# A fixed issue order on TensorE, and a pinned copy, in a decoder trunk of two layers

## The chip, the cores and the metric

The kernel runs on one core of one Trainium2 chip. The time is device microseconds of one execution. A core has TensorE (PE in the profile, with its weight loads as PEld), VectorE (DVE), ScalarE (ACT), GpSimd (POOL) and SyncE (SP), each with an instruction queue of its own.

## The reference

The kernel computes two pre-norm residual layers and a final norm on 256 tokens of width 2048, in float32. Layer 0 projects to an RWKV-7 group of 16 heads of 64 and to a differential-attention group of 8 heads, and layer 1 is a gated MLP that mixes positions in chunks of 128. Each is followed by a SwiGLU FFN of width 5632. Cut to what matters here:

```python
for i in range(DEPTH):
    h = rms_norm(x, mix_norm[i])
    if i % 2 == 0:
        z = h @ ev_w_in[j]
        y_a = rwkv7_time_mix(z[..., :RWKV_COLS], ...)
        y_b = diff_attention(z[..., RWKV_COLS:], ...)
        y = jnp.concatenate([y_a, y_b], axis=-1) @ ev_w_out[j]
    else:
        z = h @ od_w_in[j]
        y = chunked_sgu(z, ...) @ od_w_out[j]
    x = x + y
    x = x + swiglu(rms_norm(x, ffn_norm[i]), ...)
return rms_norm(x, final_norm)

def step(S, inp):                       # the scan in rwkv7_time_mix, per token
    r_t, w_t, k_t, v_t, a_t, b_t = inp
    sa = einsum('bhvk,bhk->bhv', S, a_t)
    S = S * w_t + sa[..., None] * b_t + v_t[..., None] * k_t
    return S, einsum('bhvk,bhk->bhv', S, r_t)
```

## The kernel before

**Main matmuls.** All weights come as a stream in the order of `stream()`. `weights()` (L241) loads the next piece on SP's queue and splits it into `hi` (a cast on ScalarE, L255) and `lo` (the rest, on VectorE, L256), one piece ahead of its use in the text, into five buffers each. `proj_a` (L288) multiplies 256 rows by 256 columns at a time, in layer 0's input projection with matmuls of 256 columns (L314 to L316), elsewhere with 512 and 256 (L302, L306). `proj_b` (L327) turns the operands round, in steps of 128 rows with six matmuls of 416 or 512 columns (L335 to L337).

**Side work.** The RWKV group is worked in four quarters of four heads (`quarter`, L537), written as a Python generator; rotary positions, attention, the mixing matrices and the layer norm of layer 1 are generators too. After each step of a projection `tick()` (L272) advances the generators, 1.3 steps a tick for the quarters and 1.1 for the others. So the text of the program interleaves main matmuls with small steps, and `pause(n)` puts n empty steps in between. The lines of a quarter in their order: LoRA products L545 and L546; norm of k through L562; its transposes L582; products of a chunk L619; a round trip of 16x16 diagonal blocks through DRAM on POOL's queue (L626 out, L628 back into `DB`, L629 sets ones); the bonus product L636; masks L647 and L654; transposes of v L668 and a product L681; thirteen empty steps; then the substitution that inverts the diagonal blocks on VectorE, from the copy L692 into `inv` over 15 rounds of a product L696 (`sub`) and a sum L697; the products L705 to L718 that use it; the scan over four chunks (L742, L747, L754); and the output norm with L805 and L811. L380 and L387 are the sums over partitions and the transposes of a token norm (`Norm.end`), with the Newton steps of `rsqrt` (L176) between them on VectorE. `norm.end(True)`, at L476 and L985, issues both; without `True` only the sums are issued.

**What sets the order.** The program is written in the Tile framework. A planner at compile time orders each engine's queue by an estimate of when operands are there: of what it believes ready it takes the instruction that comes first in the text. On each engine the order is then fixed, and an instruction that has to wait on the chip holds back those behind it. Before, all five queues are ordered like this.

Of the kernel before, what the change touches and what calls it, by code (L numbers as in the profile page):

```python
# [130 lines left out]
def trunk_kernel(  # L131
# [15 lines left out]
    nc = tc.nc  # L147
    V, S, T, G = nc.vector, nc.scalar, nc.tensor, nc.gpsimd

    cpool = ctx.enter_context(tc.tile_pool(name="cpool", bufs=1))  # L150
    wpool = ctx.enter_context(tc.tile_pool(name="wpool", bufs=4))
    pool = ctx.enter_context(tc.tile_pool(name="pool", bufs=1))
# [17 lines left out]
    def small(shape, tag, bufs=2):  # L170
        return pool.tile(list(shape), F32, tag=tag, name=nm(tag), bufs=bufs)
# [21 lines left out]
    def bc(ap, axis, n):  # L193
        a = ap.unsqueeze(axis)
        shape = list(a.shape)
        shape[axis] = n
        return a.to_broadcast(shape)

    def r3(ap, k):
        return ap.rearrange("p (k f) -> p k f", k=k)  # L200
# [33 lines left out]
    def cc(name):  # L234
        i, o, w = CON[name]
        return ctile[i][:, o : o + w]
# [300 lines left out]
    def quarter(q, r_, k_, v_):  # L537
# [151 lines left out]
        yield from pause(Y7)  # L689

        inv = r3(small([128, 128], "inv", 1), 8)
        V.tensor_copy(inv, bc(cc("i16"), 1, 8))  # L692
        d4 = diag.rearrange("p (u r s) -> p u r s", u=8, r=16)
        for r in range(1, 16):
            t = r3(small([128, 128], "sub"), 8)[:, :, 0 : r + 1]
# [230 lines left out]
    def ap_(g, i):  # L926
# [3 lines left out]
        else:  # L930
            res[g, i] = []
            start(f"r{g}{i}", rope(t, res[g, i]))

    start("q0", quarter(0, *rkv(0, acc)))
    ap_(0, 0)
    start("q1", quarter(1, *rkv(1)))
    ap_(0, 1)
    ap_(0, 2)
    start("q2", quarter(2, *rkv(2)))
    start("q3", quarter(3, *rkv(3)))  # L940
    for i in range(3):
# [191 lines left out]
```

## Time and profile before

| | us |
|---|---|
| median of 3 runs (2349.5 to 2353.93) | 2350.4 |
| profiled execution | 2349.51 |
| its span | 2347.7 |
| TensorE busy in it | 2291.3 |
| VectorE busy in it | 1531.8 |
| ScalarE busy in it | 1197.4 |
| mean granted TensorE clock in it | 0.992 |

A busy time is the union of an engine's instructions. A wait is the idle time of an engine in front of an instruction, put down to the semaphore that came last. A timeline row has the start and the length of a run of like instructions, then `output<-inputs` by the program's names, and in brackets the idle time before it. The clock is a share of TensorE's full clock, of whose two levels (1.2 and 2.4 GHz) the windows show a mean. The input projection of layer 0 runs until about 530 us of the span, its output projection and FFN to about 1280, and layer 1 thereafter.

### The profile page before, as it was taken

The numbers are of one execution on the slowest core, as the hardware profiler recorded it, in microseconds if no ns is written. First come the engines' busy times: TensorE is split into PE (matmuls) and PEld (weight loads), VectorE is DVE, ScalarE is ACT, GpSimd is POOL, SyncE is SP. The second block draws the span as 40 slices with busy tenths as digits, with TensorE's granted clock in tenths as the row PEclk, the third lists the DMA queues.
The fourth block names the chain that finished last, engine by engine and source line by source line (L and its number), as shares of the span: only waits on it lengthen the run. The fifth ranks groups of instructions, "written<-read, shape, count | busy, mean of one in ns | idle before, by whom it ended". The sixth has DMA issues, their size and how long they took to land.

```text
span 2347.7 us, 39701 instructions
## 1 busy us (share of the span) xinstructions
PE 2291.3 (98%) x14878; PEld 2008.8 (86%) x14878; DVE 1531.8 (65%) x2845; ACT 1197.4 (51%) x2230; POOL 66.4 (3%) x96
## 2 busy tenths in 40 slices
PE   8898989899999999999999999999999999999997
PEld 8887887688888888888888888888888888888887
DVE  7667776688766666665555558776666666665554
ACT  6445544556555555554444455555555555544443
POOL 0000000002000000000000000010000000000000
PEclk9999999999999999999999999999999999999999
DMA  6544344435566665656666765566666666656664
GB/s 217 144 135 123 117 124 146 115 113 185 183 189 189 188 189 188 189 189 188 189 189 188 244 194 176 177 188 181 192 190 189 187 188 191 190 189 189 189 189 135
DMA packets 121105, 414.08 MB, mean 176 GB/s; under 512 B 14160, under 2 KB 18384, under 8 KB 120400
## 3 DMA queue, kind: packets, MB, share of 16 engines
q1 hardware_dynamic: 113664, 401.00, 55.1%
q0 software_dynamic: 2112, 4.46, 0.9%
q10 hardware_dynamic: 5136, 6.09, 0.8%
q8 instruction: 116, 1.90, 0.3%
q14 instruction: 77, 0.63, 0.1%
HBM read 409.14 MB, written 2.36 MB: 175 GB/s over the span
## 4 chain that ended last, share of the span: by engine, by line
PE 77%; DVE 2%; issue 1%; DMA 1%; ACT 0%; POOL 0%; DVEq 0%; POOLq 0%; ACTq 0%
PE acc L302 46%; PE acc L306 24%; PE acc L314 1%; PE acc L315 1%; PE acc L316 1%; PE acc L337 1%; PE acc L336 1%; PE acc L335 1%; DVE lo L256 1%; ACT hi L255 0%; DMA AT<-in_w_s 0%; PE sm L1026 0%; DMA st<-in_wts 0%; PE sm L742 0%; DVE xres L1043 0%
## 5 line engine op out<-in xcount | busy, mean ns | idle before, releaser
L256 DVE TENSOR_TENSOR lo<-st,hi 128x512 fp32r<-128x512 f32 (+1 forms) x1520 | 1048.6, 694 | 618.6 <-ACT hi L255 613.8
L255 ACT CAST hi<-st 128x512 fp32r<-128x512 f32 (+1 forms) x1520 | 927.3, 618 | 947.3 <-PE acc L302 606.6
L302 PE MATMUL acc<-H,hi 128*128 128x512 f32 x3560 | 901.2, 393 | 0.0
L302 PEld LDWEIGHTS acc<-H,hi 128*128 128x128 f32 x3560 | 639.2, 189 | 113.3 <-issue 0.3
L306 PEld LDWEIGHTS acc<-H,lo 128*128 128x128 f32 x3560 | 486.2, 190 | 44.4 <-DVE lo L256 9.3
L306 PE MATMUL acc<-H,lo 128*128 128x256 f32 x3560 | 501.5, 283 | 9.1 <-DVE lo L256 9.1
L316 PE MATMUL acc<-H,lo 128*128 128x256 f32 x488 | 141.7, 290 | 14.6 <-DVE lo L256 14.5
L314 PE MATMUL acc<-H,hi 128*128 128x256 f32 x488 | 144.1, 295 | 8.4 <-ACT hi L255 8.4
L315 PE MATMUL acc<-H,hi 128*128 128x256 f32 x488 | 140.9, 289 | 0.0
L336 PE MATMUL acc<-lo,H 128*128 128x512 f32 (+1 forms) x320 | 126.1, 394 | 6.5 <-DVE lo L256 6.5
L335 PE MATMUL acc<-hi,H 128*128 128x512 f32 (+1 forms) x320 | 129.6, 405 | 0.0
L337 PE MATMUL acc<-hi,H 128*128 128x512 f32 (+1 forms) x320 | 125.7, 393 | 0.0
L316 PEld LDWEIGHTS acc<-H,lo 128*128 128x128 f32 x488 | 96.1, 197 | 15.9 <-DVE lo L256 15.5
L302 PE MATMUL acc<-AT,hi 128*128 128x512 f32 x400 | 105.7, 396 | 0.0
L314 PEld LDWEIGHTS acc<-H,hi 128*128 128x128 f32 x488 | 96.0, 197 | 11.2 <-ACT hi L255 8.4
L302 PE MATMUL acc<-RB,hi 128*128 128x512 f32 x392 | 101.7, 392 | 0.0
L324 DVE TENSOR_TENSOR TR<-acc,TA 128x512 f32<-128x512 f32 x96 | 66.0, 688 | 54.3 <-ACT TA L323 54.3
L315 PEld LDWEIGHTS acc<-H,hi 128*128 128x128 f32 x488 | 96.0, 197 | 0.6 <-issue 0.3
L323 ACT COPY TA<-acc 128x512 f32<-128x512 f32 x96 | 56.1, 584 | 60.6 <-PE acc L302 60.6
L302 PEld LDWEIGHTS acc<-AT,hi 128*128 128x128 f32 x400 | 72.0, 189 | 13.7 <-issue 0.3
L302 PEld LDWEIGHTS acc<-RB,hi 128*128 128x128 f32 x392 | 70.5, 189 | 12.8
L336 PEld LDWEIGHTS acc<-lo,H 128*128 128x128 f32 x320 | 61.1, 191 | 17.4 <-DVE lo L256 6.9
(330 smaller groups left out, 2057.4 us busy)
## 6 DMA issues: line engine op xcount, KB each, us to landing
st<-in_wts SPq DMA_DIRECT2D x740, 512.0 KB, 3.6
st<-in_wts SPq DMA_DIRECT2D x20, 256.0 KB, 2.7
DB<-scr POOLq DMA_DIRECT2D x4, 1024.0 KB, 13.7
st<-in_wts SPq DMA_DIRECT2D x8, 416.0 KB, 3.3
xres<-in_x SPq DMA_DIRECT2D x8, 256.0 KB, 5.8
RB<-in_rows ACTq DMA_DIRECT2D x8, 256.0 KB, 6.1
AT<-in_b_s ACTq DMA_DIRECT2D x4, 256.0 KB, 6.4
AT<-in_w_s ACTq DMA_DIRECT2D x4, 256.0 KB, 8.2
```

The lines of the kernel that those rows point to most:

```text
L255: S.copy(hi[:, :n], half)
L256: V.tensor_sub(lo[:, :n], half, hi[:, :n])
L302: T.matmul(acc[:, m, :], hi, acts[2 * u + k], start=first and k == 0, stop=last and k == 1)
L306: T.matmul(acc[:, m, 0:256], lo, acts[2 * u + k][:, 0:256], start=False, stop=False)
L314: T.matmul(acc[:, m, 0:256], hi, act[:, 0:256], start=first and k == 0, stop=False)
L315: T.matmul(acc[:, m, 0:256], hi, act[:, 256:512], start=False, stop=False)
L316: T.matmul(acc[:, m, 0:256], lo, act[:, 0:256], start=False, stop=last and k == 1)
L323: S.copy(t3, acc[:, :nmt, 256:512])
L324: V.tensor_add(dst, acc[:, :nmt, 0:256], t3)
L335: T.matmul(acc[:, t, :ncol], xh, hi, start=k == 0, stop=False)
L336: T.matmul(acc[:, t, :ncol], xh, lo, start=False, stop=False)
L337: T.matmul(acc[:, t, :ncol], xl, hi, start=False, stop=k == last)
```

## The change

TensorE's queue is no longer ordered by the planner: inside the kernel its instructions are issued in the order in which the text gives them. The other four queues are ordered by the planner as before. And the copy into `inv` with which the substitution starts is pinned behind the VectorE instruction that precedes it in the text (a `lo` cast), in VectorE's queue; this is an order of issue, not a wait. No operation is added or removed.

```diff
@@ -147,6 +147,7 @@
     nc = tc.nc
     V, S, T, G = nc.vector, nc.scalar, nc.tensor, nc.gpsimd
 
+    ctx.enter_context(tc.manual_schedule(engines={mybir.EngineType.PE}))
     cpool = ctx.enter_context(tc.tile_pool(name="cpool", bufs=1))
...
@@ -689,7 +690,7 @@
         yield from pause(Y7)
 
         inv = r3(small([128, 128], "inv", 1), 8)
-        V.tensor_copy(inv, bc(cc("i16"), 1, 8))
+        tc.keep_in_program_order(V.tensor_copy(inv, bc(cc("i16"), 1, 8)))
         d4 = diag.rearrange("p (u r s) -> p u r s", u=8, r=16)
```

## Rows read from the trace of the kernel before

**Rows 1.** The page: span and busy time, by engine, with shares and instructions.

```profile
span 2347.7 us, 39701 instructions
...
PE 2291.3 (98%) x14878; PEld 2008.8 (86%) x14878; DVE 1531.8 (65%) x2845; ACT 1197.4 (51%) x2230; POOL 66.4 (3%) x96
```

**Rows 2.** Waits, whole span: who waited for whom, us, times, longest.

```profile
ACT hi L255 <- PE acc L315: 72.0, 76, 5.4
...
PE acc L316 <- DVE lo L256: 14.5, 3, 7.8
...
PE acc L306 <- DVE lo L256: 9.1, 1, 9.1
...
PE acc L336 <- DVE lo L256: 6.5, 1, 6.5
```

**Rows 3.** Groups by line, the product: busy us, mean ns, idle us before.

```profile
L696 DVE TENSOR_TENSOR sub<-DB,inv 128x16 f32<-128x16 f32 (+14 forms) x60 | 14.0, 233 | 48.8 <-POOL DB L629 47.5
```

**Rows 4.** Timeline of POOL and VectorE at the first quarter's diagonal block.

```profile
93.59 0.62 POOL L628 DMA_DIRECT2D DB<-scr  x1 [3.12 <-DMA scr<-RB]
106.82 0.31 POOL L629 MEMSET DB<- 128x128 f32 x1 [12.61 <-DMA DB<-scr]
...
107.17 0.17 DVE L696 TENSOR_TENSOR sub<-DB,inv 128x16 f32<-128x16 f32 x1 [11.73 <-POOL DB L629]
...
114.05 0.69 DVE L256 TENSOR_TENSOR lo<-st,hi 128x512 fp32r<-128x512 f32 x1
```

**Rows 5.** Timeline of TensorE around the first stall.

```profile
103.08 0.28 PE L315 MATMUL acc<-H,hi 128*128 128x256 f32 x1
111.11 0.58 PE L316 MATMUL acc<-H,lo 128*128 128x256 f32 x1 [7.75 <-DVE lo L256]
...
114.69 0.41 PE L314 MATMUL acc<-H,hi 128*128 128x256 f32 x1
114.90 0.40 PE L315 MATMUL acc<-H,hi 128*128 128x256 f32 x1
...
115.26 0.28 PE L314 MATMUL acc<-H,hi 128*128 128x256 f32 x1
115.38 0.28 PE L315 MATMUL acc<-H,hi 128*128 128x256 f32 x1
```

**Rows 6.** Windows: length, busy by engine (instructions), clock, DMA share, GB/s.

```profile
100.00:125.00 25.00, 17.25 (x131) 17.05 (x130) 16.78 (x47) 9.27 (x18) 0.31 (x1) 0.86 0.44 138
...
225.00:250.00 25.00, 23.46 (x233) 21.58 (x232) 21.37 (x60) 14.91 (x40) 0.00 (x0) 1.00 0.51 156
```

**Rows 7.** Timeline of TensorE at the first token norm (L476).

```profile
42.56 1.02 PE L380 MATMUL sm<-TA,c 128*128 128x256 f32 x4
...
51.18 0.61 PE L387 MATMUL sm<-c,rb 128*128 128x1 f32 x4 [0.17 <-DVE rb L191]
```

**Rows 8.** Groups by line, VectorE's casts from 43.7 to 51.2 us.

```profile
L256 DVE TENSOR_TENSOR lo<-st,hi 128x512 fp32r<-128x512 f32 x5 | 3.4, 686 | 1.1 <-ACT hi L255 1.1
```

**Rows 9.** Timeline of TensorE in the first and the last quarter.

```profile
78.95 0.34 PE L335 MATMUL acc<-hi,H 128*128 128x416 f32 x1
...
88.06 1.02 PE L636 MATMUL sm<-TR,c 128*128 128x512 f32 x2
...
423.09 0.39 PE L335 MATMUL acc<-hi,H 128*128 128x512 f32 x1
...
433.81 1.02 PE L636 MATMUL sm<-TR,c 128*128 128x512 f32 x2
```

**Rows 10.** Groups by line, VectorE's casts from 72 to 88 us.

```profile
L256 DVE TENSOR_TENSOR lo<-st,hi 128x416 fp32r<-128x416 f32 (+1 forms) x11 | 6.6, 597 | 1.0 <-ACT hi L255 1.0
```

**Rows 11.** Timeline of TensorE and VectorE in the first quarter's scan.

```profile
144.95 0.45 PE L754 MATMUL sm<-sb,QQ 64*64 64x64 f32 x8
...
145.45 0.29 DVE L756 TENSOR_TENSOR ut<-sm,RB 128x128 f32<-128x128 f32 x1 [1.62 <-PE sm L754]
...
146.00 0.45 PE L747 MATMUL sm<-ut,RB 64*64 64x64 f32 x8
```

## Prediction

> **What bounds the kernel now.** I read the busy table first, then the waits of TensorE (PE), then the timeline of each stall. TensorE is busy for 2291.3 of 2347.7 us [rows 1]. The page warns that a busy PE isn't PE at its peak, so I also looked at the distances between the starts of matmuls: for the same operands they are the same all through the span, except behind a stall. So TensorE is the bound, nothing catches up later what it loses, and the change can only act through the time in which TensorE stands or runs at its lower clock.
>
> That time lies in four places. PE stands for VectorE's `lo` casts for 14.5 us at L316, 9.1 at L306 and 6.5 at L336 [rows 2]; less 0.8 at the start of the span these are 29.3 us in four stalls, one for each quarter. The timeline says why. VectorE stands 11.73 us in front of the first `sub` product, which needs the diagonal block `DB`; that load was issued at 93.59, and POOL has stood 12.61 us for it when it lands [rows 4]. Behind the product, VectorE's queue holds casts whose inputs are there. TensorE uses up what has been cast, starts its last matmul at 103.08 and the next at 111.11 [rows 5]. Over the four quarters VectorE loses 47.5 us in this way [rows 3], and TensorE 29.3 of them.
>
> Each stall costs a second time. In the window with the first one the mean granted clock is 0.86 [rows 6], and so it is in the windows with the three others. From 111.11 to 115.26 matmuls of 256 columns start every 0.21 us, at the lower of the two levels, and then every 0.12 [rows 5]. Half of these 4.15 us is lost, 2.1 us; for four stalls I take 8.4.
>
> **Part 1, the pin.** It removes no instruction and adds no wait on a semaphore; it fixes an issue order on VectorE. The copy L692 needs only a constant, so before it stands far ahead of its place, and the first products behind it stand where the planner believes `DB` to have landed. Pinned, it follows the cast that precedes it in the text, which ran at 114.05 [rows 4], and all products follow the copy through `inv`. Without the stall of 8 us that cast would come at about 106, and `DB` is ready at 107.1 by the same rows. But in the text's order (part 2) TensorE issues the products that feed the block earlier among the main matmuls, and stands some 5 us in the stretch behind them. So I expect a margin of about 5 us in the first quarter, and more in the others, where the text puts a longer stretch of matmuls between L619 and the copy. Queued behind the copy is the substitution: 60 products of 0.233 us for all quarters [rows 3] and as many sums of that length, so 7 us of VectorE in a quarter, against over 10 us of matmuls until L705 reads the result. **Gain: 29.3 + 8.4 = 37.7 us**, with 30 and 40 as bounds. Late next is VectorE itself: it has 21.37 busy us in the 25 behind the second stall [rows 6], and takes back work there that now fits into the stall. I take 2 us of cost for that (0 to 6).
>
> **Part 2, TensorE in the order of the text.** Before, main matmuls whose operands are there pass a side step that isn't ready. Afterwards they queue behind it, so each such place costs what the step is late against its place in the text. Nothing runs ahead meanwhile: the casts need buffers that TensorE releases, and ScalarE's wait up to 5.4 us for it at L315 [rows 2]. There are three kinds of place.
>
> (a) The two `norm.end(True)`, L476 and L985. In the text the transposes L387 directly follow the sums L380. Before, PE ends L380 at 43.58 and starts L387 at 51.18 [rows 7], and 62 main matmuls run between; the second place shows the same chain. Meanwhile VectorE works off the Newton steps, with casts of 0.69 us among them: five in the window, the first already running when the chain starts [rows 8]. With TensorE standing the other four can't come. Each put the chain off by 0.69 us at most; since steps that need one another leave gaps, I take 0.5. The bare chain is then 7.6 - 4 x 0.5 = 5.6 us, and each place costs 5.6 to 7.6 us of standing. The shortest stall of before that brought the clock down was 6 us, so I add 2.4 us of lower clock (0 to 3). **2 x 8.0 = 16 us** (11 to 21).
>
> TensorE's rule of order is weighed here. L387 waits 0.17 us for VectorE [rows 7], and in that time no main matmul starts. The Trainium skill, "TensorE: Matmul & The Clock Gate", section "Step-by-step: what each phase is for", says that only weight loads are pulled ahead: "The MATMULs themselves stay in program order". By that rule all of part 2 is paid; could matmuls pass a waiting one, the sum would be 37.7 us faster. The trace agrees with the rule.
>
> (b) The fronts of the four quarters, from the LoRA products (L545, L546) to the bonus product L636. The text puts nine yields between them; at 1.3 steps a tick these are six or seven ticks, in the first quarter 42 matmuls. That place in the text is 78.95, and L636 ran at 88.06, 9.1 us late. In the last quarter it is 423.09 against 433.81, 10.7 us [rows 9]. The two between are 6.8 and 5.1 late by the same reading; the four make 31.7. This is the upper bound. For the lower one I take away all casts that VectorE put among the steps of the chain, 6.6 us in the first quarter [rows 10]; with 2.5 us left in each, 10 remain. Casts go on wherever main matmuls run between the steps, so I take the middle: **20 us** (10 to 32).
>
> (c) The rest: steps of the scan, of attention and of the output norm that a few matmuls passed. In the first such place L754 starts at 144.95, VectorE's addition ends at 145.74, and L747 starts at 146.00, behind four main matmuls [rows 11]; in the text's order TensorE would stand some 0.4 us. I count 17 of them, each 0.3 to 2.0 us late against the end of what stands before it, 13 us together. With fewer casts in the way I take **11 us** (8 to 14). Two small places elsewhere (the transposes L473, the first mixing product L1026) add an estimated 2.5 (1 to 4). In the FFN and the output projections the order of before already is that of the text.
>
> **The sum.** 16 + 20 + 11 + 2.5 + 2 - 37.7 = +14 us. The profiled execution took 2349.5 us (the span of 2347.7 and 1.8 around it), 0.9 under the median of the runs, 2350.4. So 2364.
>
> **The rivals.** Rival A, the waits in the text's order are short, and it ends faster. While TensorE stands, VectorE and ScalarE have only the chain to do, so each front costs its lower bound, and 5.6 us don't bring the clock down. Then part 2 costs 11 + 10 + 8 + 1 = 30, and the sum is -7: 2343. It is faster from a part 2 below 33 us. For it: ScalarE's casts stop when TensorE does [rows 2]. Against it: until they stop, up to five buffers are filled between the steps.
>
> Rival B, the waits are as long as the lateness of before, and the clock falls in the four fronts too: 21 + 31.7 + 14 + 4 + 6 + 4 x 2.1 - 37.7 = +47, 2397. Against it: all falls of before stand behind stalls of 6 us and more, and a front's single waits are 1 to 4 us by the split of its lateness over four steps. The Trainium skill, same page, section "HAM oscillation — how this bites in real kernels", tells of a kernel that fell to the lower clock at each of its repeated waits; by that B would be the likelier one, and no row of before shows it for short waits.
>
> Rival C, the pin doesn't do what it says, as `DB` lands behind the pinned place: two stalls of about 4 us remain, with their clock: +14 + 12, 2376.
>
> **How the numbers follow.** The forecast (2352 to 2378) has 0.55, A (2335 to 2351) 0.25, B (over 2379) 0.13, C 0.07. A measurement of this kernel can tell about 0.2%, 4.7 us, from no change. Three fifths of A lie below 2345.7: faster 0.15. The rest of A and the forecast up to 2355 are same, 0.2. Slower is 0.65. The range leaves out the lower end of A and the upper part of B: 2342 to 2387.
>
> **What would show it.** The pin is right if VectorE's wait in front of `sub` and PE's waits for `lo` are gone from the list. Part 2 is right if PE stands for VectorE at L387 twice, for 5 to 8 us, and at L562, L582, L619 and L636 for 1 to 4 us each. If PE's new waits sum to under 33 us, A holds; if the fronts' windows show a granted clock under 1, B. I am wrong altogether if PE's idle time grows in the FFN, or if `sub` still waits for POOL.

## The result and the profile after

The changed kernel takes 2373.9 us (median of 4 runs, 2369.85 to 2374.96) against 2350.0 for the kernel before, measured beside it: a ratio of 1.0099, with an interval of 1.0077 to 1.0121. It is slower, as forecast, and 10 us above the predicted 2364, inside the range. The profiled execution took 2374.09 us. In the changed kernel the lines behind the inserted one have numbers higher by one (L388 is L387 of before, L583 is L582, L697 is L696).

The page of the changed kernel, span and busy time, beside [rows 1]:

```profile
span 2372.3 us, 39704 instructions
...
PE 2302.7 (97%) x14878; PEld 2017.8 (85%) x14878; DVE 1536.1 (65%) x2845; ACT 1200.7 (51%) x2230; POOL 65.3 (3%) x96
```

Two subtractions already split the loss. Span less TensorE's busy time, called standing below, was 2347.7 - 2291.3 = 56.4 us and is now 69.6: 13.2 more. And the same 14878 matmuls are busy for 11.4 us longer: that is the clock. The two make the 24.6 us by which the span grew. The split is that of these two executions: the one profiled here has the lowest mean granted clock of the changed kernel's four runs (0.986, the others 0.988 to 0.990).

Waits of TensorE in the changed kernel (who waited for whom, us, times, longest), beside [rows 2]:

```profile
PE sm L388 <- DVE rb L192: 12.5, 2, 6.9
PE sm L583 <- ACT TA L568: 8.7, 4, 2.6
...
PE sm L889 <- DVE TB L885: 4.1, 3, 3.0
PE sm L563 <- ACT TR L559: 3.6, 4, 2.0
PE sm L812 <- DVE RB L798: 2.9, 3, 2.0
...
PE sm L637 <- DVE TR L635: 1.5, 3, 0.9
...
PE sm L620 <- DVE BK L594: 1.2, 2, 0.8
```

The three waits for `lo` have left the list. In their place stand the two token norms (12.5 us), the four fronts (L583, L563, L637, L620, and with them a single 0.6 at L682, a little behind the last front: 15.6 us), and many small ones, most of them of the scan, attention and the output norm (19.6 us in the whole list, against 2.0 before).

POOL and VectorE in the first quarter of the changed kernel, beside [rows 4]:

```profile
115.32 0.33 POOL L630 MEMSET DB<- 128x128 f32 x1 [13.33 <-DMA DB<-scr]
...
121.28 0.22 DVE L693 COPY inv<-con 128x128 f32<-128x128 f32 x1
```

The group of the product by line (busy us, mean ns, idle us before), beside [rows 3]:

```profile
L697 DVE TENSOR_TENSOR sub<-DB,inv 128x16 f32<-128x16 f32 (+14 forms) x60 | 13.9, 231 | 1.3
```

The pin holds. `DB` is ready at 115.65 and the copy runs at 121.28, a margin of 5.6 us where some 5 were expected. In the other quarters, where more was expected, it is 4.4, 5.8 and 12.4 us by the same reading. The 47.5 us that VectorE stood for `DB` [rows 3] are down to 1.3 in front of the whole group.

TensorE at the first token norm and in the first front of the changed kernel, beside [rows 7, 9]:

```profile
41.12 1.03 PE L381 MATMUL sm<-TA,c 128*128 128x256 f32 x4
49.06 1.01 PE L388 MATMUL sm<-c,rb 128*128 128x1 f32 x4 [6.92 <-DVE rb L192]
...
50.30 0.41 PE L316 MATMUL acc<-H,hi 128*128 128x256 f32 x1
50.51 0.41 PE L317 MATMUL acc<-H,lo 128*128 128x256 f32 x1
...
76.38 0.48 PE L546 MATMUL sm<-lw,sk 64*128 64x256 f32 x1
...
79.56 1.23 PE L563 MATMUL sm<-c,TR 128*128 128x2 f32 x8 [0.72 <-ACT TR L559]
...
81.49 0.35 PE L337 MATMUL acc<-lo,H 128*128 128x416 f32 x1
81.67 0.35 PE L338 MATMUL acc<-hi,H 128*128 128x416 f32 x1
...
82.42 0.55 PE L338 MATMUL acc<-hi,H 128*128 128x416 f32 x1
82.76 0.55 PE L336 MATMUL acc<-hi,H 128*128 128x416 f32 x1
...
86.58 1.11 PE L583 MATMUL sm<-c,TA 128*128 128x128 f32 x4 [2.58 <-ACT TA L568]
```

Both kinds of place are seen here. At the norm nothing runs between L381 and L388 any more, and the matmuls behind start every 0.21 us, at the lower level. In the front matmuls of 416 columns start 0.19 us apart until 81.67 and 0.35 apart from 82.42. So the clock fell before the wait of 2.58 us. What lies ahead of the fall is the LoRA products on 64 of the 128 rows (L546 and L547, from 76.38), a wait of 0.72 us and eight products of 2 columns, with matmuls of 416 columns between them.

Windows of the changed kernel (length, busy by engine, granted clock, DMA share, GB/s), beside [rows 6]:

```profile
25.00:50.00 25.00, 17.62 (x138) 16.91 (x136) 16.38 (x36) 9.39 (x19) 0.00 (x0) 0.89 0.58 187
50.00:75.00 25.00, 25.00 (x192) 25.00 (x192) 14.62 (x26) 13.15 (x26) 0.00 (x0) 0.91 0.41 132
75.00:100.00 25.00, 20.79 (x128) 17.24 (x127) 17.58 (x51) 10.78 (x22) 4.33 (x8) 0.80 0.33 98
...
175.00:200.00 25.00, 22.16 (x106) 16.31 (x106) 19.67 (x64) 12.29 (x25) 0.00 (x0) 0.93 0.43 134
...
250.00:275.00 25.00, 22.14 (x298) 19.95 (x300) 15.40 (x40) 9.85 (x29) 0.00 (x0) 0.93 0.35 107
...
300.00:325.00 25.00, 20.35 (x138) 17.98 (x137) 18.91 (x62) 11.84 (x24) 0.00 (x0) 0.92 0.37 118
325.00:350.00 25.00, 24.61 (x268) 22.70 (x268) 16.17 (x31) 13.53 (x28) 4.78 (x9) 0.94 0.49 119
...
425.00:450.00 25.00, 20.71 (x126) 15.52 (x126) 18.39 (x52) 9.24 (x17) 4.42 (x9) 0.86 0.32 93
...
500.00:525.00 25.00, 23.17 (x249) 18.55 (x248) 17.00 (x50) 10.10 (x32) 0.00 (x0) 0.93 0.24 79
...
1350.00:1375.00 25.00, 19.40 (x76) 15.75 (x75) 13.54 (x26) 9.50 (x15) 0.00 (x0) 0.86 0.35 109
```

These are all windows under 1 before the end of the span. The first two and the last belong to the norms. The falls at the four fronts are in those from 75, 175, 325 (it begins at the end of the window before) and 425 us. The three others aren't fronts: there the matmuls slow down behind a wait of 3.0 us in attention (L889, at 251.5), one of 2.0 in an output norm (L812, at 306.4) and one of 1.5 in the scan (L748, at 507.4).

### The profile page after: what moved, and what is told of

Read it like the earlier page. It is cut to its first block, busy times and chain, and to the rows that moved or that the text cites. A ratio compares the mean times of both kernels' runs of the same rounds, so it can differ in the third digit from the quotient of the medians.

```text
span 2372.3 us, 39704 instructions
## 1 busy us (share of the span) xinstructions
PE 2302.7 (97%) x14878; PEld 2017.8 (85%) x14878; DVE 1536.1 (65%) x2845; ACT 1200.7 (51%) x2230; POOL 65.3 (3%) x96
## 3 DMA queue, kind: packets, MB, share of 16 engines
HBM read 409.14 MB, written 2.36 MB: 173 GB/s over the span
## 4 chain that ended last, share of the span: by engine, by line
PE 76%; DVE 1%; ACT 0%; DMA 0%; issue 0%; DVEq 0%; ACTq 0%
PE acc L303 45%; PE acc L307 23%; PE acc L315 1%; PE acc L316 1%; PE acc L317 1%; PE acc L336 1%; PE acc L337 1%; PE acc L338 1%; DVE lo L257 1%; ACT hi L256 0%; DMA AT<-in_w_s 0%; PE sm L1027 0%; PE sm L743 0%; DVE xres L1044 0%; PE sm L381 0%
## 5 line engine op out<-in xcount | busy, mean ns | idle before, releaser
L303 PE MATMUL acc<-H,hi 128*128 128x512 f32 x3560 | 901.4, 393 | 0.0
L303 PEld LDWEIGHTS acc<-H,hi 128*128 128x128 f32 x3560 | 638.7, 189 | 113.0 <-issue 0.3
L316 PE MATMUL acc<-H,hi 128*128 128x256 f32 x488 | 141.2, 289 | 0.0
L336 PE MATMUL acc<-hi,H 128*128 128x512 f32 (+1 forms) x320 | 134.4, 420 | 0.0
L338 PE MATMUL acc<-hi,H 128*128 128x512 f32 (+1 forms) x320 | 127.1, 397 | 0.0
L303 PE MATMUL acc<-AT,hi 128*128 128x512 f32 x400 | 104.9, 395 | 0.0
L303 PE MATMUL acc<-RB,hi 128*128 128x512 f32 x392 | 101.7, 392 | 0.0
L316 PEld LDWEIGHTS acc<-H,hi 128*128 128x128 f32 x488 | 96.9, 199 | 0.1
L303 PEld LDWEIGHTS acc<-AT,hi 128*128 128x128 f32 x400 | 72.0, 189 | 13.7 <-ACT hi L256 0.3
L303 PEld LDWEIGHTS acc<-RB,hi 128*128 128x128 f32 x392 | 70.5, 189 | 12.8
L336 PEld LDWEIGHTS acc<-hi,H 128*128 128x128 f32 x320 | 62.8, 196 | 13.9 <-issue 1.2
```

The costliest lines, as they stand in the source:

```text
L303: T.matmul(acc[:, m, :], hi, acts[2 * u + k], start=first and k == 0, stop=last and k == 1)
L316: T.matmul(acc[:, m, 0:256], hi, act[:, 256:512], start=False, stop=False)
L336: T.matmul(acc[:, t, :ncol], xh, hi, start=k == 0, stop=False)
L338: T.matmul(acc[:, t, :ncol], xl, hi, start=False, stop=k == last)
```

## The experiments

All times are medians beside runs of the kernel before, which took 2350.6 to 2351.0 us.

| kernel | us | ratio to before | span | PE busy | standing |
|---|---|---|---|---|---|
| pin alone (e1) | 2327.0 | 0.9902 (0.9885 to 0.9920) | 2330.7 | 2289.9 | 40.8 |
| order alone (e2) | 2398.0 | 1.0201 (1.0184 to 1.0218) | 2395.7 | 2308.9 | 86.8 |
| changed, norms early (e3) | 2354.5 | 1.0013 (1.0004 to 1.0022) | 2350.5 | 2291.5 | 59.0 |
| changed, fronts spread (e4) | 2363.4 | 1.0053 (1.0038 to 1.0068) | 2361.4 | 2296.3 | 65.1 |
| pin, half the block (e5) | 2311.5 | 0.9827 (0.9810 to 0.9843) | 2310.1 | 2282.1 | 28.0 |
| pin, order behind layer 0 (e7) | 2341.2 | 0.9956 (0.9941 to 0.9971) | 2338.4 | 2292.3 | 46.1 |
| changed, both repairs (e8) | 2347.1 | 0.9986 (0.9977 to 0.9996) | 2347.5 | 2293.8 | 53.7 |
| pin, block in four pieces (e9) | 2336.4 | 0.9940 (0.9925 to 0.9955) | 2334.7 | 2290.9 | 43.8 |
| pin, deeper weights (e6) | 2322.0 | 0.9884 (0.9868 to 0.9901) | 2320.0 | 2286.6 | 33.4 |

The spans, busy times and waits are those of one execution each. That of the pin alone took 2332.5 us, the slowest of its four runs (2324.4 to 2332.5), so its waits are rather at the upper end.

**The two parts alone.** Only the pin:

```diff
-        V.tensor_copy(inv, bc(cc("i16"), 1, 8))
+        tc.keep_in_program_order(V.tensor_copy(inv, bc(cc("i16"), 1, 8)))
```

> The copy pinned, TensorE ordered by the planner as before. My theory (two opposite parts that add up: the pin gains the four stalls and their clock, the text's order costs more): VectorE's wait for DB goes or falls to a few us, PE's waits for lo (29.3 us) go, no window before the end under a granted clock of 1, 2350 - 38 = 2312 us, up to 2318 if the landing is only just in time, since without the text's order the block is produced later among the main matmuls. Rival (the pin needs the text's order of TensorE to have its landing in time): VectorE still waits 5 us and more in at least two quarters, and the time is 2325 to 2345.

Only the order:

```diff
+    ctx.enter_context(tc.manual_schedule(engines={mybir.EngineType.PE}))
```

> TensorE in the order of the text, the copy not pinned. My theory (the parts add): the four stalls of before stay (VectorE waits 40 to 50 us for DB) and the waits of the text's order come on top, 2374 + 38 = 2412 us. Rival (TensorE's waits for the side steps give DB the time to land, so the two stalls of a quarter overlap): VectorE waits under 25 us for DB, 2380 to 2395.

The pin alone gives 24.0 us, not the 32 to 38 of the theory. The time lies in the rival's range, but not for the rival's reason, as VectorE doesn't wait for `DB`; and against the expectation three windows fall under a granted clock of 1 (0.93, 0.93 and 0.86, from 100, 325 and 425 us). The order alone costs 47.0, less than the theory's 62 and a little more than the rival's. On top of the order the pin gives 2398.0 - 2373.9 = 24.1, and on top of the pin the order costs 2373.9 - 2327.0 = 46.9. So the parts add, and the pin is worth less than I expected on either path. The reasons differ. Order alone, waits of VectorE for `DB` and of TensorE for `lo`:

```profile
DVE sub L697 <- POOL DB L630: 41.0, 4, 13.7
...
PE acc L317 <- DVE lo L257: 7.8, 5, 3.3
PE acc L337 <- DVE lo L257: 6.3, 2, 5.2
...
PE acc L307 <- DVE lo L257: 2.0, 2, 1.0
```

VectorE stands almost as long as before, but TensorE only 15.3 us for it (the sum of these waits, less 0.8 at the start of the span) instead of 29.3 [rows 2]. So in the text's order less is left for the pin to win. Pin alone, waits of TensorE over the span, then the longest of ScalarE's for weights, in the third block load:

```profile
PE acc L314 <- ACT hi L255: 12.5, 3, 8.5
PE sm L888 <- DVE TB L884: 6.8, 4, 4.7
PE acc L335 <- ACT hi L255: 3.2, 1, 3.2
...
ACT hi L255 <- DMA st<-in_wts: 9.0, 1, 9.0
```

With the pin VectorE no longer holds the casts back, and then the next thing is late: the weights. Of the 12.5 us at L314, 8.5 are the start of the span; the other 4.0, the 3.2 at L335 and most of the 6.8 at L888 (1.8 before) are new. In the stretches of the four block loads ScalarE waits 7.3, 7.9, 9.0 and 4.6 us for weight pieces, 28.8 together. The DMA issues of the pin alone (count, KB each, median us to landing), over the span and then in the stretch of the third block, show them beside the block:

```profile
st<-in_wts SPq DMA_DIRECT2D x740, 512.0 KB, 3.6
...
st<-in_wts SPq DMA_DIRECT2D x4, 512.0 KB, 11.4
DB<-scr POOLq DMA_DIRECT2D x1, 1024.0 KB, 16.6
```

A piece that usually lands in 3.6 us takes 11.4 while this block of 1 MB loads (7.4 to 10.0 beside the other three), though the two are on different queues. The Trainium skill, "DMA: Bandwidth & Descriptors", section "Issuing engines are not separate DMA queues", says that transfers of all issuing engines "run on the same 16 DMA engines and interleave with each other"; these rows agree.

**Is it the weights?** Three kernels with the pin alone ask that. First, half of the block; the other half is set to zero, so the inverses of half of the blocks are left out:

```diff
-        nc.gpsimd.dma_start(diag, bc(scr.rearrange("g u r s -> g (u r s)"), 1, 16))
+        nc.gpsimd.dma_start(diag[:, 0:1024], bc(scr.rearrange("g u r s -> g (u r s)")[:, 0:1024], 1, 16))
+        G.memset(diag[:, 1024:2048], 0.0)
```

> The pin alone, with half of the diagonal block loaded: the other half of DB is set to zero on POOL, so that the inverses of half of the blocks are left out; all other work stays. The pin alone took 2327.0 us, 24 less than before where 37.7 were expected. Theory (weights): while the whole block of 1 MB loads for some 14 to 16 us, the weight pieces come late (ScalarE waits 7.3, 7.9, 9.0 and 4.6 us for them in the four quarters, 28.8 together), TensorE runs out of casts and stands, and the clock falls; with half the bytes the load lands in some 8 us, ScalarE's waits for weights in the four stretches fall under 15 us together, TensorE's waits for hi at L314 and L335 go or fall under 2 us, and the time is 2315 to 2322. Rival (the products that use the inverse, or VectorE, are what costs the rest): the load is hidden anyway, and the time stays at 2325 to 2330.

It took 2311.5 us, 15.5 less than the pin alone and somewhat less than the theory said. In the four block loads ScalarE waits 6.1 us for weights, 2.7 at the longest, and the list of TensorE's waits begins so:

```profile
PE acc L314 <- ACT hi L255: 8.3, 1, 8.3
PE sm L974 <- DMA AT<-in_w_s: 3.2, 1, 3.2
```

The 8.3 is the start of the span; L335 and the two other waits at L314 are gone. The standing is 28.0, 28.4 under before, and the busy time is 9.2 under before: this is the 29.3 + 8.4 of the prediction's part 1. So that gain is there, if the block's load costs nothing. But half a block takes two things away. It holds the weights up less, and it lands earlier. The copy in the first quarter of this kernel, and the end of the whole block's load with the pin alone:

```profile
104.56 0.22 DVE L693 COPY inv<-con 128x128 f32<-128x128 f32 x1
...
108.13 0.31 POOL L629 MEMSET DB<- 128x128 f32 x1 [14.43 <-DMA DB<-scr]
```

With the weights in time the pinned copy comes at 104.56, and a whole block that lands as late as with the pin alone would make VectorE stand again. With the pin alone this doesn't show, because the late weights hold back the casts, and with them the copy, to 109.63. So the 15.5 us are what the load of the second half costs; how much of them is weights and how much a landing that would be late isn't parted by this run.

Second, one more buffer for weight pieces, for room paid with one less for each of `hi` and `lo`:

```diff
-                st = wpool.tile([128, 1024], F32, tag="st", name=nm("st"), bufs=3)[:, :n]
+                st = wpool.tile([128, 1024], F32, tag="st", name=nm("st"), bufs=4)[:, :n]
...
-            hi = wpool.tile([128, 512], F32R, tag="hi", name=nm("hi"), bufs=5)
-            lo = wpool.tile([128, 512], F32R, tag="lo", name=nm("lo"), bufs=5)
+            hi = wpool.tile([128, 512], F32R, tag="hi", name=nm("hi"), bufs=4)
+            lo = wpool.tile([128, 512], F32R, tag="lo", name=nm("lo"), bufs=4)
```

> The pin alone, with four buffers for weight pieces instead of three, and for the room of it four buffers instead of five for hi and for lo. Theory (weights come late while the block loads): a fourth piece in store covers some 4 us of each shortage, ScalarE's waits for weights in the four stretches fall from 28.8 us to about 15, and the time from 2327 to 2316 to 2323. Rival (what TensorE lives on in the shortage is the store of cast tiles, which is now one less): 2327 to 2335.

2322.0 us, inside the theory's range: 5 less than the pin alone, though the runs of the two overlap (2320.8 to 2326.5 here), and the fastest kernel here that loads the whole block. In the four stretches ScalarE's waits for weights fall from 28.8 us to 12.8, over the span from 62.6 to the 17.3 of this row:

```profile
ACT hi L255 <- DMA st<-in_wts: 17.3, 8, 6.9
```

Third, the same block in four pieces, each issued when the one before has landed:

```diff
-        nc.gpsimd.dma_start(diag, bc(scr.rearrange("g u r s -> g (u r s)"), 1, 16))
-        G.memset(r3(diag, 8)[:, :, 0:256:17], 1.0)
+        for o in range(0, 2048, 512):
+            tc.keep_in_program_order(nc.gpsimd.dma_start(diag[:, o : o + 512], bc(scr.rearrange("g u r s -> g (u r s)")[:, o : o + 512], 1, 16)))
+            tc.keep_in_program_order(G.memset(r3(diag[:, o : o + 512], 2)[:, :, 0:256:17], 1.0))
```

> The pin alone, with the whole diagonal block loaded in four pieces of 256 KB, each issued when the one before has landed. The bytes are the same; between two pieces lies the latency of one, in which the weights have the DMA engines to themselves. The pin alone took 2327.0 us, and with half of the bytes 2311.5. Theory (it is the burst that starves the weights): ScalarE's waits for weights in the four stretches fall from 28.8 us to 15 or less, and the time to 2315 to 2322, if the block, which then lands some 2 to 6 us later, is still there when the pinned copy runs. Rival (it is the bytes, or VectorE stands for the later block): 2325 to 2335.

2336.4: the rival's outcome, by its second reason. ScalarE's single waits for weights are 3.4 us at most. But from the first issue to the end of POOL's wait the block now takes 18.9, 21.7, 22.5 and 20.1 us in the four quarters, against 15.1, 16.1, 16.7 and 14.2 with the pin alone. It lands behind the pinned place, and the old stall is back:

```profile
PE acc L316 <- DVE lo L256: 5.2, 2, 3.2
...
DVE sub L697 <- POOL DB L630: 24.7, 4, 7.4
```

TensorE stands 5.2 us for it at L316 and 2.6 at L336. This is also what rival C of the prediction looks like.

**What the order costs, place by place.** The sums of both norms issued earlier in the text of the changed kernel, so that main matmuls stand between them and the transposes (`columns()` holds the transposes; `mid` is called after the eighth step):

```diff
+    norm.end()
     acc = proj_a("w_in", 0, 256, act, False)
-    norm.end(True)
+    norm.columns()
...
-        acc = proj_b("od_in", range(KT // 2), D + 512 * n, act)
+        acc = proj_b("od_in", range(KT // 2), D + 512 * n, act, mid=norm.end if n == 0 else None)
...
-            norm.end(True)
+            norm.columns()
```

> The changed kernel, with the sums of the two token norms issued earlier in the text (before the projection ahead of the first, in the middle of the one ahead of the second) and the transposes where they were. My theory (each of the two places costs 5.6 us of standing and about 2.9 us of work at the lower clock behind it): PE's wait at the transposes is gone, 11.2 + 5.8 = 17 us less than the changed kernel, 2357 us. Rival (the clock falls there because of the waits in the quarters, or the time is given back in the next wait): 11 us less or fewer, 2363 or above.

2354.5: 19.5 us come back, and L388 leaves the list of waits. Of the span's 21.8 us, 10.6 are standing (69.6 to 59.0) and 11.2 busy time, that is, clock. Not all of this clock is that of the norms. Two windows of this kernel:

```profile
50.00:75.00 25.00, 23.94 (x170) 22.20 (x168) 15.76 (x40) 13.53 (x28) 0.00 (x0) 0.93 0.54 156
...
175.00:200.00 25.00, 21.00 (x163) 15.48 (x164) 21.87 (x59) 11.80 (x23) 4.47 (x9) 1.00 0.30 93
```

The longest wait of the second front, 2.36 us, lies in the window from 175 us in both kernels, and the clock is 1.00 here and 0.93 in the changed kernel. So a wait of this length brings the clock down in one kernel and not in another. The first front lies 10 us earlier than in the changed kernel. There the clock falls again behind the wait of 0.72 us (matmuls of 416 columns start 0.35 us apart from 72.04 on), so that fall didn't hang on the norm's stall.

The pin alone, with the order of the text only from the FFN of layer 0 on; so of the two norms only the second is in it:

```diff
+    ctx.enter_context(tc.manual_schedule(engines={mybir.EngineType.PE}))
     norm = ffn(0, ...)
```

> The pin alone, and TensorE in the order of the text only from the FFN of layer 0 on. Of the waits that the order brought, only those at the second token norm with transposes close behind its sums (L388, 5.6 us) and at the first mixing product (L1027, 1.9 us) are in this stretch. Theory (each such wait costs its standing and its fall of the clock, about 3.4 us of work): 2327 + 5.6 + 1.9 + 3 = 2337 to 2339, and the granted clock falls under 1 in the window behind L388 alone. Rival (a wait costs its standing alone): 2333 to 2335. If the FFN or the output projections also lose by the order of the text: over 2343.

2341.2, so 14.3 us against the pin alone, 2 over the theory. Its waits in this stretch and windows behind them:

```profile
PE sm L387 <- DVE rb L191: 5.6, 1, 5.6
...
PE sm L1027 <- DVE mv L191: 1.1, 1, 1.1
```

```profile
1325.00:1350.00 25.00, 24.60 (x103) 20.42 (x104) 11.86 (x18) 12.40 (x20) 0.00 (x0) 0.92 0.50 147
...
1400.00:1425.00 25.00, 23.06 (x127) 19.95 (x127) 23.39 (x50) 11.25 (x21) 0.00 (x0) 0.93 0.42 132
```

The clock falls not only behind L387, as the theory had it, but also behind the two waits at L1027 (1.1 and 0.8 us), where the window shows 0.93, while behind the same two waits of the changed kernel it shows 1.00; and in this run it fell behind a wait of 2.8 us for a DMA at L974 (1.7 with the pin alone), which isn't of the order. The FFN and the output projections of layer 0 lose nothing by the order: no wait of TensorE and no window under 1 lies in them.

The fronts' steps put further apart in the changed kernel (more empty steps in them, three fewer behind):

```diff
-Y1 = 2
+Y1 = 4
...
-Y7 = 13
+Y7 = 10
...
-        yield
+        yield from pause(2)
```

The last line stands for three places, in front of L563, L620 and L637.

> The changed kernel with empty steps added ahead of the late side steps of a quarter's front (one ahead of L562, two more ahead of L582, one ahead of L619, one ahead of L636) and three taken from the pause ahead of the substitution. My theory (a front costs what its steps are late against their place in the text, 15.7 us of standing in the profile, and the clock that falls there costs about as much again): PE's waits in the fronts fall from 15.7 to under 5 us, the falls of the clock at the fronts go, 16 to 20 us less than the changed kernel, 2354 to 2358 us. Rival (the waits only move to the next step, which is late by as much): less than 6 us gained, 2368 or above.

2363.4, between theory and rival. The waits of this kernel:

```profile
PE sm L889 <- DVE TB L885: 6.8, 5, 3.4
PE sm L812 <- DVE RB L798: 5.2, 3, 2.6
...
PE sm L583 <- ACT TA L568: 2.4, 2, 1.2
```

L583 falls from 8.7 to 2.4 us and the waits of the fronts together from 15.6 to 5.3, nearly as the theory had it. But later steps rise: L889 and L812, and also L719 (0.9 to 2.6) and L303 (nothing to 2.3). So standing falls by 4.5 us only, and 6.4 come from the clock. Its falls at the fronts go, and new ones come behind the longer waits (windows of 0.86 from 475 and from 525 us, both at 1.00 in the changed kernel).

Both repairs in one kernel:

> The changed kernel with both repairs: the sums of the two token norms issued earlier in the text (which gave 19.5 us), and the steps of the four fronts put further apart (which gave 10.5 us). Theory (the places of part 2 are separate, each with its own standing and its own clock): the gains add, 2374 - 19.5 - 10.5 = 2344, between 2340 and 2348; TensorE's idle time falls to about 31 us. Rival (what one repair gives, later waits take back): 2350 or more, near the 2354.5 of the first repair alone.

2347.1: 26.8 us of the 30.0 that the two gave apart, inside the theory's range. TensorE's idle time, though, is 53.7 us and not the 31 expected; that is about what the two gains of standing, 10.6 and 4.5, leave of the 69.6. The two repairs add up. But even so repaired the order is 20 us behind the pin alone.

## Why the prediction was right, and where its sizes were off

The sign, the range and the places of the standing held. The profiled executions, set against the terms of the sum:

| term, us | predicted | measured |
|---|---|---|
| TensorE's standing for `lo` | -29.3 | -29.3 (all gone) |
| standing at the two norms | +11.2 | +12.5 |
| standing in the fronts | +20 | +15.6 |
| the rest of part 2 (11 + 2.5) | +13.5 | +14.4 (by difference; 17.6 by the list) |
| clock: 2 x 2.4 - 8.4 | -3.6 | +11.4 (busy time) |
| VectorE crowded | +2 | in the rows above |
| sum | +13.8 | +24.6 |

**The pin** did what was said: the waits for `lo` are gone, with the margin that was worked out for the first quarter. **The norms** stand 6.9 and 5.6 us, within 5.6 to 7.6, and one cast lies in the chain of the first where there were five; e3 gave back 19.5 us for them, some clock of other places included, where I took 16. **The fronts** stand less than the middle that I took, nearer to the lower bound of 10 than to 31.7. Rival A's reason doesn't explain it: nine casts of 5.3 us in all still lie among the steps of the first front, against eleven of 6.6 [rows 10]. **The rest** came out dearer: by the list the new waits of the scan, attention, the output norm and the two small places are 17.6 us, inside the bounds (9 to 18) but 4 over the middle; waits of before that went, 1.6 us of them for a DMA at L973, hide this in the difference.

**The clock is the term that failed.** It came out 15 us dearer; the standing, crowding included, came out 4 us cheaper, and so the span missed by 10.8. The step was "a front's single waits are 1 to 4 us", so the clock falls only behind the norms. But it fell in all four fronts (0.80, 0.93, 0.94, 0.86), behind single waits of 2.6 us and less, and at three places of the scan, attention and the output norm (0.93, 0.92, 0.93), behind waits of 1.5 to 3.0 us, which no rival had priced.

An estimate from the windows, one less the clock, times 25 us, gives 8.5 us for the norms, 11.8 for the fronts and 5.5 for the three places, against 14.0 for the four stalls of before: 11.8 more, about the 11.4 of the busy time. The estimate counts standing at the lower clock too, most of all at the norms. Behind the first norm the matmuls go at the lower level from 49.94 to 54.56 us, so 2.3 us are lost where I took 2.4. So the norms were sized about right, and the fronts and the three places are the miss.

The part of rival B on the clock came true, while its other part, waits as long as the lateness of before, didn't. The page that spoke for B, the Trainium skill, "TensorE: Matmul & The Clock Gate", section "HAM oscillation — how this bites in real kernels", tells of a clock that falls anew at each repeated wait; the windows of the changed kernel agree for its fronts, and they show it for shorter single waits, among small products, than any stall of before. But e3, with the same wait in the second front, shows 1.00 there, so it isn't each wait that has this price.

**"Late next is VectorE itself"** failed too, and the time alone didn't show it. With the pin alone late next are the weights, which the block's own load holds up. Half of that load costs 15.5 us (e5), where I took 2; e6 and e9 hold the shortage down and get back 5 us and nothing, the second because its block lands late. In the changed kernel the shortage hardly appears: ScalarE waits at most 4.4 us for a piece in any of the block loads there. That TensorE's waits in the fronts let the stores fill first would be a reason, but two traces speak against it: in e4 and e8 the fronts' waits are down to 5.3 us, and ScalarE waits for no piece in any block load. Why the text's order spares the weights stays open. It fits with the order costing only 47 us on top of the pin, though its own waits, with the clock, come to more: it gives back a shortage that the pin alone pays. Without the pin it gives back 14 of the 29.3 us that TensorE stood for `lo` (e2).

## What to carry to other kernels

When a stall is taken away, look for what lay hidden under it: here a load that ended at the same moment also held up the weight stream, and over a third of the expected gain stayed there until the load was halved; a deeper store for the stream brought back 5 us. An issue order fixed by the text turns side steps that are late into waits (in the fronts 15.6 us for a lateness of 31.7), so put distance between a step and its reader in the text before fixing the order, and price such places with the clock as a range, short waits too. And measure each part of a change by itself: this one joined a gain of 24 us with a loss of 47, and the pin with a deeper weight store (2322.0 us) beats both kernels.

## What was not expected of the hardware

- The granted clock fell behind LoRA products on 64 rows, a single wait of 0.72 us and eight products of 2 columns (at about 82 us of the changed kernel, and again in e3), and in the kernel with the order behind layer 0 the window with two waits of 1.1 and 0.8 us shows 0.93. All falls of before, up to its end, stood behind stalls of 6 us and more.
- The same waits don't always do it: behind a wait of 2.36 us the window shows 0.93 in the changed kernel and 1.00 in e3, and behind those of 1.1 and 0.8 us it shows 1.00 in the changed kernel.
- One broadcast load of 1 MB on POOL's queue stretches the 512 KB weight pieces of SP's queue from 3.6 us until landing to between 7.4 and 11.4 in its stretch, with the pin alone.
- Four pieces of 256 KB in a row, each issued when the one before has landed, take 3.8 to 5.9 us longer than 1 MB at once beside the same stream.
